# Combining the two softmax maps of a differential attention on GpSimd, in two instructions, instead of in one of VectorE

## The chip, the core and the metric

The kernel runs on one core of a Trainium2 chip. The core has a matrix engine (TensorE, PE in the profile, with its weight loads as PEld), three elementwise engines (VectorE or DVE, ScalarE or ACT, GpSimd or POOL) and SyncE (SP), which issues DMAs. TensorE writes to PSUM, which has eight banks; GpSimd works on SBUF only. The metric is the device time of one execution in microseconds (us).

## The reference, cut to what matters

One encoder block on 1024 tokens of width 1024, in float32: an input projection, two attentions side by side, gates, an output projection and an MLP. The change lies in the second attention, the differential one, with 4 heads. Its core, for each block of 128 queries:

```python
sc = jnp.einsum('bqhcd,bkhcd->bhcqk', qb, k).astype(jnp.float32) * scale
p = jax.nn.softmax(sc, axis=-1)
pd = p[:, :, 0] - lam * p[:, :, 1]
return jnp.einsum('bhqk,bkhe->bqhe', pd.astype(v.dtype), v)
```

So there are two maps of 128 queries by 1024 keys per head and block, and one is subtracted from the other with a factor before the product with the values. The heads' outputs are normalised afterwards.

## The kernel before, in words

Products are made in halves: a float32 matrix is split into a high part, which TensorE takes, and the low part that remains, and a product is three products of such parts. Making a low part is one elementwise subtraction, and which engine makes it is written in the code.

The program has stages, one behind the other: input projections, the differential attention, the dilated attention, the gates and the output projection, and the MLP in two stages. The differential attention is one loop over 34 steps, in which 4 heads of 8 query blocks each are worked on with a lag:

- `b_scores` (lines 688 to 703) makes the scores of both maps of block n on TensorE, `sb` in the rows (line 697), in a PSUM tile of two banks; there are two such tiles. VectorE takes the minimum of each row, `mn` (line 700; the sign of the scores is turned), and ScalarE the exponential, `p` (line 702), which also sums the row into `zz`.
- `b_combine` (lines 705 to 712), one step later, takes the reciprocals of the sums, `zi` (line 710), the ratio `rr` of the two sums with the factor lambda (line 711), and adds the second map, times that ratio, to the first (line 712). The map is thus left with the scale of the first sum; the normalisation later takes the reciprocal into account.
- `b_values` (lines 714 to 726), two steps later, transposes the combined map on TensorE in eight pieces, `tb` (line 724), into two PSUM tiles. `split_T` makes the high part on ScalarE (line 622) and the low part on VectorE (line 623), `pt`. Every second block `b_products` multiplies the values with the parts of two blocks, `ob` (lines 735 to 737), which ScalarE copies out (line 738).
- `fill`, at every second step, adds a piece of other work: half of a gate's projection (`gate_first`, lines 625 to 646). A weight is loaded (`wgf`), split into a high part by ScalarE (line 253) and a low part by GpSimd (line 254, `wa_g_l`), multiplied (line 245, `g`), and GpSimd adds the result to three stored parts (line 641, `gq`), on which ScalarE takes a tanh.
- `b_norm`, once a head, has a small step on GpSimd (lines 164 and 165), and near the end GpSimd makes the low halves of the next stage's weights (line 150, `wb_l`).

The order in which each engine's instructions stand is not that of the text: a scheduler places all instructions of the program, by its own estimate of their durations, and puts in the waits. Each engine then goes through its queue strictly in that order. So a changed instruction can also change where its neighbours stand, on every engine and in SP's queue of loads.

The maps `p` are in a pool of 9 tiles, the transposed parts `pt` in one of 7.

Of the kernel before, what the change touches and what calls it, by code (L numbers as in the profile page):

```python
# [14 lines left out]
ALU = mybir.AluOpType  # L15
# [68 lines left out]
def tile_hybrid_block(ctx: ExitStack, tc: tile.TileContext, t: dict, out: bass.AP):  # L84
    nc = tc.nc
# [511 lines left out]
    def tiny(tag, name, w=8, bufs=2):  # L597
        return p2.tile([P, w], F32, tag=tag, name=name, bufs=bufs)
# [106 lines left out]
    def b_combine(o, qb):  # L705
        h = o.h
        pm, zz = o.p[qb], o.zz[qb]

        r = tiny("rr", f"rr{h}_{qb}", 1, 4)
        nc.vector.reciprocal(o.zi[:, qb, :], zz)  # L710
        nc.vector.scalar_tensor_tensor(r, zz[:, 0:1], lam, o.zi[:, qb, 1:2], op0=ALU.mult, op1=ALU.mult)
        nc.vector.scalar_tensor_tensor(pm[0], pm[1], r, pm[0], op0=ALU.mult, op1=ALU.add)

    def b_values(o, qb):
        h, pr, u = o.h, qb // 2, qb % 2
# [225 lines left out]
    for n in range(len(steps) + LAG):  # L941
        if n < len(steps):
            h, qb = steps[n]
            if qb == 0:
                heads[h] = b_open(h)
            b_scores(heads[h], qb)
        if n % 2:
            fill()

        if n == 28:  # L950
            ah[0] = a_open(0)
        if n == 30:
            ah[1] = a_open(1)
        if 0 < n <= len(steps):
            h, qb = steps[n - 1]
            b_combine(heads[h], qb)
        later()
        if n >= LAG:
            h, qb = steps[n - LAG]
            defer(b_values(heads[h], qb))  # L960
            if qb == NT - 1:
                defer(partial(b_close, heads.pop(h)))
# [440 lines left out]
```

## Time and profile before

| | us |
|---|---|
| median of 3 runs | 1702.39 |
| lowest and highest | 1696.20, 1707.07 |
| the profiled execution | 1701.56 |
| its span, from first to last instruction | 1699.8 |

Busy time is what an engine spent in instructions that compute; several engines are busy at once, so the shares don't add up to one. A wait is the time that an engine was idle before an instruction, put down to what released it.

### The profile page before, as it was taken

How to read it: one execution, taken by the hardware profiler on the slowest of the kernel's cores; microseconds unless marked ns; L12 is line 12 of the kernel's file. 1: busy time of each engine (PE TensorE's matmuls, PEld its weight loads, DVE VectorE, ACT ScalarE, POOL GpSimd, SP SyncE). 2: the span in 40 equal slices, each digit the busy share in tenths (PEclk: the TensorE clock that was granted, in tenths of full speed). 3: DMA queues.
4: the chain of work that ended last, by engine and by line, in shares of the span. 5: the costliest groups of instructions: out<-in, count | busy, mean ns of one | idle time of the engine just before them, and what ended most of it. 6: DMA issues, size and time to landing. Idle time of an engine off the chain costs nothing. (4 is left out here: it accounts for less than half of the span.)

```text
span 1699.8 us, 22314 instructions
## 1 busy us (share of the span) xinstructions
PE 1569.3 (92%) x8216; PEld 1324.2 (78%) x8216; DVE 1230.8 (72%) x1560; ACT 709.4 (42%) x1176; POOL 712.4 (42%) x412
## 2 busy tenths in 40 slices
PE   7899989998889998999999998999999888999997
PEld 6798767776677778899879996777888677777776
DVE  5876788689688996555546548544344899999995
ACT  4432222222567774445422336345444643333322
POOL 1634545455223241112120016333333498888771
PEclk8999999999899998999999999999999999999999
DMA  6366576555855658665475432433332632222212
GB/s 203 130 207 211 169 227 227 166 179 175 267 192 191 230 192 276 186 203 187 144 250 184 137 96 73 147 120 115 113 112 93 248 137 99 99 100 99 87 38 99
DMA packets 211869, 272.36 MB, mean 160 GB/s; under 512 B 12304, under 2 KB 146608, under 8 KB 211760
## 3 DMA queue, kind: packets, MB, share of 16 engines
q1 hardware_dynamic: 207152, 254.16, 46.0%
q10 hardware_dynamic: 4608, 16.78, 2.5%
q8 instruction: 65, 1.06, 0.3%
q14 instruction: 44, 0.36, 0.1%
HBM read 184.86 MB, written 80.27 MB: 156 GB/s over the span
## 5 line engine op out<-in xcount | busy, mean ns | idle before, releaser
L1291 PE MATMUL p<-wb_h,fa_h 128*128 128x512 f32 x392 | 157.1, 402 | 21.5 <-DVE xb L1301 8.1
L1292 PE MATMUL p<-wb_l,fa_h 128*128 128x512 f32 x392 | 155.8, 397 | 4.2 <-DVE wb_l L1249 4.2
L1293 PE MATMUL p<-wb_h,fa_l 128*128 128x512 f32 x392 | 155.3, 397 | 0.0
L1291 PEld LDWEIGHTS p<-wb_h,fa_h 128*128 128x128 f32 x392 | 74.9, 191 | 44.4 <-issue 14.5
L1249 POOL TENSOR_TENSOR wb_l<-ws,wb_h 128x512 fp32r<-128x512 f32 x54 | 86.0, 1603 | 17.3 <-ACT wb_h L1248 17.3
L1292 PEld LDWEIGHTS p<-wb_l,fa_h 128*128 128x128 f32 x392 | 75.5, 193 | 20.7 <-DVE wb_l L1249 5.2
L1293 PEld LDWEIGHTS p<-wb_h,fa_l 128*128 128x128 f32 x392 | 75.3, 192 | 16.5 <-DVE fa_l L1249 0.5
L702 ACT ACTIVATE p<-sb,mn 128x1024 f32<-128x1024 f32 x64 | 71.4, 1117 | 38.3 <-DVE mn L700 24.1
L697 PE MATMUL sb<-kb,qb 128*128 128x512 f32 x256 | 74.7, 416 | 13.1 <-ACT p L702 7.6
L700 DVE TENSOR_REDUCE mn<-sb 128x1 f32<-128x1024 f32 x64 | 76.7, 1216 | 11.0 <-PE sb L697 10.7
L1249 POOL TENSOR_TENSOR wb_l<-w2r,wb_h 128x512 fp32r<-128x512 f32 x48 | 78.7, 1660 | 13.7 <-ACT wb_h L1248 13.7
L164 POOL TENSOR_SCALAR n_y<-n_ss 128x1 f32<-128x1 f32 x23 | 6.0, 261 | 186.1 <-ACT n_xn L171 183.1
L273 DVE TENSOR_TENSOR s<-w 128x512 f32<-128x512 f32 x15 | 13.5, 901 | 97.2 <-DMA w<-in_w_ff 97.2
L254 POOL TENSOR_TENSOR wt_f_l<-w,wt_f_h 128x1024 fp32r<-128x1024 f32 x15 | 36.1, 2408 | 91.6 <-ACT wt_f_h L253 91.6
L1248 ACT ACTIVATE fa_h<-fs 128x512 fp32r<-128x512 f32 x56 | 35.1, 627 | 84.9 <-issue 40.9
L1249 DVE TENSOR_TENSOR fa_l<-fs,fa_h 128x512 fp32r<-128x512 f32 x56 | 70.4, 1264 | 0.0
L811 PE MATMUL sa<-kh_a,zq 128*128 128x256 f32 x256 | 69.2, 301 | 0.0
L1248 ACT ACTIVATE fa_h<-fr 128x512 fp32r<-128x512 f32 x50 | 31.2, 626 | 90.7 <-PE p L1292 52.2
L836 DVE TENSOR_TENSOR pta<-ta,pta 128x512 fp32r<-128x512 f32 x64 | 43.8, 688 | 33.7 <-ACT pta L835 33.4
L697 PEld LDWEIGHTS sb<-kb,qb 128*128 128x128 f32 x256 | 46.4, 194 | 25.4 <-ACT p L702 11.2
L811 PE MATMUL sa<-kl_a,zq 128*128 128x256 f32 x256 | 66.1, 289 | 0.0
L1142 ACT ACTIVATE c<-c 128x512 f32<-128x512 f32 x64 | 39.6, 623 | 56.2 <-DVE c L300 50.1
(500 smaller groups left out, 5272.1 us busy)
## 6 DMA issues: line engine op xcount, KB each, us to landing
w<-in_w_in SPq DMA_DIRECT2D x32, 512.0 KB, 4.2
qk<-r ACTq DMA_DIRECT2D x32, 512.0 KB, 4.5
f<-c SPq DMA_DIRECT2D x64, 256.0 KB, 4.6
w2r<-in_w_ff SPq DMA_DIRECT2D x32, 512.0 KB
fr<-f SPq DMA_DIRECT2D x32, 512.0 KB, 6.2
w<-in_w_ff SPq DMA_DIRECT2D x30, 512.0 KB
vb<-vb SPq DMA_DIRECT2D x16, 512.0 KB, 6.9
rot<-raw SPq DMA_DIRECT2D x64, 128.0 KB, 3.8
```

Source lines behind the costliest of these rows:

```text
L254: eng.tensor_tensor(lo[:, :n, :], x, f(hi[:, :n, :]), op=ALU.subtract)
L697: nc.tensor.matmul(sps[:, 512 * n:512 * n + 512], q[:, z, (qb % 4) * P:(qb % 4 + 1) * P], o.k[m][:, 512 * n:512 * n + 512], start=z == 0, ...
L700: nc.vector.tensor_reduce(mn, sps, axis=AX.X, op=ALU.min)
L702: nc.scalar.activation(p, sps, AF.Exp, scale=-1.0, bias=mn, accum_out=o.zz[qb][:, m:m + 1])
L811: nc.tensor.matmul(ps[:, 0:CM], zq[:, n % 4, c, :], kk[:, c * CM:(c + 1) * CM], start=c == 0 and kk is o.kh, stop=c == NCLS - 1 and kk is ...
L836: nc.vector.tensor_tensor(view[1], tv, f(view[0]), op=ALU.subtract)
L1142: nc.scalar.activation(c, c, AF.Relu)
L1248: nc.scalar.activation(hi, x, AF.Copy)
L1249: eng.tensor_tensor(lo, x, f(hi), op=ALU.subtract)
L1291: nc.tensor.matmul(acc, ah[:, c], bh, start=i == 0, stop=False)
L1292: nc.tensor.matmul(acc, ah[:, c], bl, start=False, stop=False)
L1293: nc.tensor.matmul(acc, al[:, c], bh, start=False, stop=i == len(ops) - 1)
```

## The change

The one VectorE instruction of `b_combine` that multiplies the second map by the ratio and adds the first becomes two on GpSimd: the second map is multiplied by the ratio in place, and then the two maps are added into the first. The reciprocals and the ratio stay on VectorE.

```diff
         nc.vector.scalar_tensor_tensor(r, zz[:, 0:1], lam, o.zi[:, qb, 1:2], op0=ALU.mult, op1=ALU.mult)
-        nc.vector.scalar_tensor_tensor(pm[0], pm[1], r, pm[0], op0=ALU.mult, op1=ALU.add)
+        nc.gpsimd.tensor_scalar(pm[1], pm[1], r, None, op0=ALU.mult)
+        nc.gpsimd.tensor_tensor(pm[0], pm[0], pm[1], op=ALU.add)
```

In the rows of the order, lines behind 712 are higher by one in the changed kernel. Names have the block and the map or part in them: `p_5_0` is the first map of block 5, `rr_5` its ratio, `zi` the reciprocals of the head.

VectorE's queue in the second head, where the ratios of blocks 5 and 6 stand. Before:

```order
L711 SCALAR_TENSOR_TENSOR rr_5_4337<-zz_5_4256,lam,zi_3895 128x1
L712 SCALAR_TENSOR_TENSOR p_5_0_4264<-p_5_1_4273,rr_5_4337,p_5_0_4264 128x1024
L768 SCALAR_TENSOR_TENSOR eb_3639<-eb_3639,gsub,rrow_4165 128x1024
L623 TENSOR_TENSOR pt_1_0_1_4239<-tb_2_0_4242,pt_1_0_0_4238 128x4x128
L700 TENSOR_REDUCE mn_6_0_4324<-sb_6_0_4319 128x1
L772 TENSOR_TENSOR obl_4206<-eb_3639,obh_4205 128x1024
L623 TENSOR_TENSOR pt_1_1_1_4241<-tb_2_1_4249,pt_1_1_0_4240 128x4x128
```

And with the change:

```order
L700 TENSOR_REDUCE mn_6_1_4346<-sb_6_1_4341 128x1
L710 RECIPROCAL zi_3902<-zz_5_4268 128x2
L711 SCALAR_TENSOR_TENSOR rr_5_4350<-zz_5_4268,lam,zi_3902 128x1
L710 RECIPROCAL zi_3902<-zz_6_4331 128x2
L711 SCALAR_TENSOR_TENSOR rr_6_4443<-zz_6_4331,lam,zi_3902 128x1
L623 TENSOR_TENSOR pt_2_0_1_4382<-tb_4_0_4385,pt_2_0_0_4381 128x4x128
L623 TENSOR_TENSOR pt_2_1_1_4384<-tb_4_1_4392,pt_2_1_0_4383 128x4x128
```

The combination is gone from the queue, and the ratio of block 5 has moved behind the minima of block 6 and stands right ahead of the ratio of block 6.

GpSimd's queue around the same blocks, from the gate additions of one gate to the weight half of the next. Before:

```order
L254 TENSOR_TENSOR wa_g_l<-wgf_4554,wa_g_h 128x1024
L641 TENSOR_TENSOR gq_4281<-gq_4281,gp_7_4285 128x512 x2
L641 TENSOR_TENSOR gq_7_4283<-gq_7_4283,gp_7_4285 128x512
L254 TENSOR_TENSOR wa_g_l<-wgf_4847,wa_g_h 128x1024
L641 TENSOR_TENSOR gq_4560<-gq_4560,gp_0_4564 128x512 x2
```

And with the change:

```order
L641 TENSOR_TENSOR gq_4293<-gq_4293,gp_7_4297 128x512 x2
L641 TENSOR_TENSOR gq_7_4295<-gq_7_4295,gp_7_4297 128x512
L712 TENSOR_SCALAR p_5_1_4285<-p_5_1_4285,rr_5_4350 128x1024
L713 TENSOR_TENSOR p_5_0_4276<-p_5_0_4276,p_5_1_4285 128x1024
L712 TENSOR_SCALAR p_6_1_4348<-p_6_1_4348,rr_6_4443 128x1024
L713 TENSOR_TENSOR p_6_0_4339<-p_6_0_4339,p_6_1_4348 128x1024
L254 TENSOR_TENSOR wa_g_l<-wgf_4867,wa_g_h 128x1024
L712 TENSOR_SCALAR p_7_1_4416<-p_7_1_4416,rr_7_4502 128x1024
```

Between the gate additions and the weight half, which stood next to each other, there are now the combinations of two blocks, in the same queue.

TensorE's queue between the transposes of blocks 4 and 5 of the second head. Before:

```order
L724 MATMUL tb_4_1_4378<-ident,p_4_0_4189 128x128 x4
L697 MATMUL sb_7_0_4386<-kb_0_3875,qb_0_1_3885 128x512
L697 MATMUL sb_7_1_4395<-kb_1_3877,qb_1_1_3888 128x512 x4
L724 MATMUL tb_5_0_4433<-ident,p_5_0_4264 128x128 x4
L245 MATMUL g_0_4565<-hB_167,wa_g_h 128x512
```

And with the change:

```order
L725 MATMUL tb_4_1_4392<-ident,p_4_0_4200 128x128 x4
L697 MATMUL sb_7_0_4400<-kb_0_3882,qb_0_1_3892 128x512 x4
L697 MATMUL sb_7_1_4409<-kb_1_3884,qb_1_1_3895 128x512 x4
L245 MATMUL g_7_4418<-hB_169,wa_g_l 128x512
L725 MATMUL tb_5_0_4448<-ident,p_5_0_4276 128x128 x4
```

Between the two blocks' transposes stood one product of the first map's scores of block 7 and four of the second; now all eight stand there, and one gate product. In the third and fourth head it is the eight score products alone.

## Rows read from the trace of the kernel before

**Rows 1.** The page, first part: busy us, share of the span, instructions of each engine.

```profile
PE 1569.3 (92%) x8216; PEld 1324.2 (78%) x8216; DVE 1230.8 (72%) x1560; ACT 709.4 (42%) x1176; POOL 712.4 (42%) x412
```

**Rows 2.** Busy time by stretch: stretch, length, busy us (instructions), clock, DMA share, GB/s.

```profile
core 0: us, PE busy (x) PEld busy (x) DVE busy (x) ACT busy (x) POOL busy (x), PEclk, DMA share, GB/s
442.00:641.00 199.00, 183.09 (x1064) 155.65 (x1063) 174.61 (x245) 144.15 (x254) 67.82 (x40) 0.96 0.62 211
...
480.00:510.00 30.00, 26.93 (x147) 22.88 (x145) 23.25 (x34) 18.11 (x33) 8.08 (x6) 0.89 0.59 198
...
570.00:600.00 30.00, 26.75 (x157) 22.57 (x156) 26.62 (x35) 21.80 (x41) 9.41 (x6) 1.00 0.57 202
600.00:641.00 41.00, 37.17 (x226) 31.96 (x224) 38.16 (x55) 31.00 (x54) 17.28 (x10) 0.94 0.66 233
```

**Rows 3.** Waits, 430 to 650 us: who waited for whom, total us, times, longest.

```profile
ACT p L702 <- DVE mn L700: 24.1, 21, 3.3
...
DVE pt L623 <- ACT pt L622: 11.3, 11, 4.0
PEld sb L697 <- ACT p L702: 11.2, 12, 3.5
```

**Rows 4.** Instructions by line and shape, 430 to 650 us: columns as shown first.

```profile
line engine op names shapes xcount | busy us, mean ns | idle before us <-releasers
...
L712 DVE SCALAR_TENSOR_TENSOR p<-p,rr,p 128x1024 f32<-128x1024 f32 x32 | 41.6, 1300 | 0.8
...
L641 POOL TENSOR_TENSOR gq<-gq,gp 128x512 f32<-128x512 f32 x24 | 36.1, 1533 | 60.9 <-ACT gp L636 60.9
...
L254 POOL TENSOR_TENSOR wa_g_l<-wgf,wa_g_h 128x1024 fp32r<-128x1024 f32 x7 | 18.3, 2614 | 46.1 <-ACT wa_g_h L253 15.9 <-DMA gate<-gp 12.0 <-PE tb L724 9.9
...
L150 POOL TENSOR_TENSOR wb_l<-wb_r,wb_h 128x1024 fp32r<-128x1024 f32 x3 | 7.7, 2563 | 11.9 <-ACT wb_h L148 11.9
...
L991 POOL MEMSET pta<- 128x512 f32 x1 | 0.5, 525 | 10.4 <-PE ob L737 10.4
```

**Rows 5.** Timeline, GpSimd: start us, us, instruction [idle before, releaser].

```profile
443.48 3.77 POOL L641 TENSOR_TENSOR gq<-gq,gp 128x512 f32<-128x512 f32 x3 [17.35 <-ACT gp L636]
450.66 2.39 POOL L254 TENSOR_TENSOR wa_g_l<-wgf,wa_g_h 128x1024 fp32r<-128x1024 f32 x1 [3.41 <-ACT wa_g_h L253]
...
559.23 0.25 POOL L164 TENSOR_SCALAR nb_y<-bms 128x8 f32<-128x8 f32 x1 [9.36 <-DVE bms L756]
559.56 1.68 POOL L165 TENSOR_TENSOR nb_y<-nb_y,mhalf 128x8 f32<-128x8 f32 x1
```

**Rows 6.** Timeline, ratios on VectorE and what ran beside three of them.

```profile
484.61 1.06 ACT L253 ACTIVATE wa_g_h<-wgf 128x1024 fp32r<-128x1024 f32 x1 [4.10 <-DMA wgf<-in_w_in]
...
485.74 2.36 POOL L254 TENSOR_TENSOR wa_g_l<-wgf,wa_g_h 128x1024 fp32r<-128x1024 f32 x1 [11.98 <-DMA gate<-gp]
...
486.79 1.33 DVE L711 SCALAR_TENSOR_TENSOR rr<-zz,lam,zi 128x1 f32<-128x1 f32 x1
...
487.30 2.07 PE L697 MATMUL sb<-kb,qb 128*128 128x512 f32 x4 [3.07 <-ACT p L702]
...
492.40 0.22 DVE L711 SCALAR_TENSOR_TENSOR rr<-zz,lam,zi 128x1 f32<-128x1 f32 x1
...
617.89 2.40 POOL L150 TENSOR_TENSOR wb_l<-wb_r,wb_h 128x1024 fp32r<-128x1024 f32 x1 [5.67 <-ACT wb_h L148]
...
618.95 1.36 DVE L711 SCALAR_TENSOR_TENSOR rr<-zz,lam,zi 128x1 f32<-128x1 f32 x1
...
629.47 2.93 POOL L150 TENSOR_TENSOR wb_l<-wb_r,wb_h 128x1024 fp32r<-128x1024 f32 x1 [1.69 <-ACT wb_h L148]
...
630.72 1.70 DVE L711 SCALAR_TENSOR_TENSOR rr<-zz,lam,zi 128x1 f32<-128x1 f32 x1
```

**Rows 7.** Timeline, eight score products of TensorE in a row.

```profile
501.04 2.08 PE L697 MATMUL sb<-kb,qb 128*128 128x512 f32 x8
```

**Rows 8.** Timeline, the end of the stage.

```profile
635.81 1.06 ACT L148 ACTIVATE wb_h<-wb_r 128x1024 fp32r<-128x1024 f32 x1 [3.87 <-DMA wb_r<-in_w_branch_b]
...
640.03 1.28 DVE L712 SCALAR_TENSOR_TENSOR p<-p,rr,p 128x1024 f32<-128x1024 f32 x1
...
641.17 1.05 PE L724 MATMUL tb<-ident,p 128*128 128x128 f32 x4
```

## The prediction

> **What bounds the kernel now.** I read the page's first part [rows 1]: TensorE is busy for 92% of the span, VectorE for 72%, GpSimd for 42%. Those are averages over stages, and the change touches one stage alone, the 32 query blocks of the differential attention. So the second view is busy time by stretch. All 32 combinations lie between 442 and 641 us; in these 199 us TensorE is busy 183.09, VectorE 174.61, ScalarE 144.15 and GpSimd 67.82 [rows 2]. TensorE has 15.91 us idle in it; three of the stretches, 480 to 510, 570 to 600 and 600 to 641, hold 3.07, 3.25 and 3.83 of that. The stage is close to TensorE's work, with VectorE nearly as full behind it, and GpSimd has two thirds of its time free.
>
> The third view is the waits. The exponentials waited 24.1 us for VectorE's minima, and TensorE's weight loads of the scores then waited 11.2 us for exponentials to free their banks; VectorE in turn waited 11.3 us for ScalarE [rows 3]. So a shorter VectorE queue is worth something, at most TensorE's idle time. One piece is not VectorE's: at 484.61 us ScalarE had stood 4.10 us behind the load of a weight, and TensorE's scores then waited 3.07 us [rows 6]. That leaves 15.91 - 3.07 = 12.8 us.
>
> **What is removed.** 32 VectorE instructions of mean 1300 ns [rows 4], 41.6 us. They stand between the minima and the low halves in VectorE's queue, so this is relief for the waits above and nothing else.
>
> **What is added.** On GpSimd 32 scalings and 32 adds of 128x1024. An add of that size with two inputs takes 2.39 us when nothing disturbs it (the weights' low half at 450.66) [rows 5]. The scaling by one value per partition has no row of its size. Bounds: the fill of 128x512 took 525 ns [rows 4], so 1.05 us for twice the columns, reading nothing; the two-input operation took 2.39. The scaling reads one stream where the add reads two and the fill none; it is nearer to the fill, and I take 1.2 us, about half the add. A combination then costs 3.6 us in place of 1.28 (the free instruction at 640.03) [rows 8].
>
> By the Trainium skill, GPSIMD Engine Reference, Engine selection, elementwise work is VectorE's, about twice as fast on two inputs, while one input runs at roughly line rate on GpSimd. Its cycle accounting gives 1.03 cycles an element for small bodies, by estimate 0.9 us at 1.2 GHz for the scaling; no run here shows it, and the sum below would have GpSimd at 83% in place of 88%.
>
> GpSimd's queue now. It holds 24 gate additions (three in 3.77 us), 7 and 3 weight halves of 2.39, and three pairs of small steps of 0.25 + 1.68 [rows 4, 5]: 30.2 + 23.9 + 5.8 = 59.9 us. With 32 x 3.6 = 115.2 it is 175.1 of 199, 88%. It fits, but only just, and this queue was free of anything urgent before.
>
> **The lock between the two engines.** The step ahead of each combination, the ratio rr on VectorE, works on one column and takes 0.22 us (492.40). Three times it did not: 1.33 us from 486.79, 1.36 from 618.95, 1.70 from 630.72 [rows 6]. Each time a GpSimd instruction ran, 485.74 + 2.36 = 488.10, 617.89 + 2.40 = 620.29, 629.47 + 2.93 = 632.40, and the ratio ended 0.02 us behind it. It stands still until GpSimd's instruction is over. Now GpSimd will be in a long instruction (32 adds and 10 halves, 100.4 us) half the time and in a short one (56 of about 1.22, 68.6 us) a third of it. A ratio that arrives at random waits half an instruction: 100.4/199 x 1.2 + 68.6/199 x 0.61 = 0.82 us, over 32 ratios 26 us. VectorE's relief shrinks from 41.6 to 15.4 us, 37%, and I count 37% of 12.8: **4.8 us less**. In the new order some ratios stand right behind each other (blocks 5 and 6 of the second head): the second meets the scaling that the first has started, and the low halves behind it wait too.
>
> The Trainium skill says in SBUF — State Buffer, Who interferes with whom, that a VectorE instruction with two SBUF inputs and a GpSimd instruction that reads SBUF exclude each other for the whole instruction. The trace agrees on the ratios (ends 0.02 us apart); the page would have no share of the waits escape, which is the third rival.
>
> **The tail.** The last block has no work behind it. Its exponential ended, its combination ran from 640.03, and transposes came at 641.17 [rows 8]. There 3.6 + 0.1 - 1.28 = **2.4 us more** is on the path (2.3 by the low bound of the scaling, 3.6 by the high one).
>
> **The queue.** GpSimd's weight halves feed gate products that TensorE takes in order. Each of the 10 now finds a combination in front of it with a chance of 115/199 = 58%, with half of 3.6 us left: 1.0 us each, 10.4 in all. TensorE has scores and values ahead of half of these, by the order: **5.2 us more**. A combination behind a gate addition or a half is later too, and each is 2.3 us longer in itself. That is covered by what TensorE has between a block's transposes and the next block's: eight score products of 2.08 us [rows 7] and a share of gate or value products. The cover is thinnest between blocks 4 and 5 of the last three heads, where one gate product or none stands beside the scores; with nothing but the scores each block would cost up to 2.3 - 2.08 = 0.2 us, some 7 us over 32, which I leave to the range.
>
> The order before and behind the stage is as it was apart from a few loads on SP's queue between this stage and the next, which I cost at nothing: GpSimd and SP wait for the last products there in any case.
>
> **Sum.** Against the profiled execution's 1701.56 us: -4.8 + 2.4 + 5.2 = +2.8, or 1704.4. That execution lies 0.8 us under the median of 1702.39, so the forecast is **1705 us**, no change that can be told: a measurement of this kernel resolves about 1%, 17 us.
>
> **Rivals.**
> *VectorE's relief comes through.* If the ratios mostly arrive while GpSimd waits for them, the whole 12.8 us can return and the queue costs nothing: 1701.6 - 12.8 + 2.4 = 1691. For it: VectorE is named in the longest wait of the stage. Against it: 88% of GpSimd, and TensorE at 92%. Chance 0.15; only with the low bound of every cost is it over 1%, so 0.06 for faster.
>
> *GpSimd becomes the bound of the stage.* Place: its queue from 442 to 641 us. It decides from the scaling's price: (199 - 59.9) / 32 = 4.35 us for a combination, so a scaling over 1.95 us. At its upper bound of 2.39 the queue holds 32 x 4.78 + 59.9 = 212.9 us, 13.9 over; with the tail's 3.6 that is 1719. With 5% of idle time, since it must wait for ratios, halves from ScalarE and loads, 224 us and 1730. A late load is now paid here too: at 635.81 ScalarE had waited 3.87 us for the weight whose low half GpSimd makes [rows 8], and in the new order one such half stands between the scaling and the add of block 5 of the last head. For it: no row shows that one input is cheaper than two, and the disturbed rows are longer (2614 ns mean of the halves, 1533 of the additions) [rows 4]. Against it: what disturbed them was above all the VectorE instruction that goes. Chance 0.22.
>
> *The lock takes back more than the change gives.* If each ratio waits a whole add, 32 x (2.39 - 0.22) = 69 us, VectorE holds 174.6 - 41.6 + 69 = 202 of the 199 us and becomes the bound itself: 1701.6 + 3 + 2.4 = 1707 with no idle time, 1720 if half of its 24 us of idle time today stays. For it: ratios side by side in the order. Against it: the ratio has to precede its own combination, so the longest instruction is often still to come. Chance 0.08.
>
> The forecast keeps 0.55. That the change doesn't do what it says is excluded: the order shows the 64 instructions on GpSimd and none left on VectorE.
>
> **Range and chances.** Low end 1690, the first rival; high end 1730, the second with its idle time. Faster by over 1%: 0.06. Slower by over 1%, above 1719: most of the second rival, part of the third, and of the forecast the case that cover and tail both go wrong, 0.28. Within 1%: 0.66.
>
> **What would show it.** In the new profile: the scaling's mean (1.2 us forecast, the case turns at 1.95); GpSimd's busy time from the first to the last combination (175 of about 200 us); the ratio's mean, 0.22 us plus 0.82, about 1.04 (2.4 for the third rival); TensorE's waits for transposes, which should now name the GpSimd add, few and at block 5 of a head and the end; the exponentials' wait for minima, which should fall from 24.1 us by a third. The prediction is wrong if the stage lasts under 190 or over 215 us, or if the difference lies outside it.

## The result, and the profile after it

The changed kernel takes 1754.46 us (median of 4 runs, 1753.00 to 1755.47); the kernel before, on the same chip, 1702.14. The ratio is 1.0308, with a 95% interval of 1.0274 to 1.0342: **slower by 3.1%**, 52 us. The forecast was 1705, with a range of 1690 to 1730. The profiled execution has a span of 1753.7 us, 53.9 more than before.

The first part of the page, which answers to [rows 1]:

```profile
PE 1590.4 (91%) x8216; PEld 1338.4 (76%) x8216; DVE 1213.4 (69%) x1528; ACT 709.1 (40%) x1176; POOL 874.1 (50%) x476
```

GpSimd has gained 161.7 us for 64 instructions, 5.05 per combination. VectorE has lost 32 instructions, but only 17.4 us of the 41.6 that they took [rows 4].

Busy time by stretch. The combinations now lie between 439 and 695 us, 256 where it was 199 [rows 2]:

```profile
439.00:695.00 256.00, 206.54 (x1089) 171.79 (x1088) 155.12 (x217) 145.18 (x257) 228.38 (x103) 0.89 0.53 176
```

For a measure with the same work on both sides I take the time from the first score product of this stage to the first of the next: 222.4 us before and 274.5 after, 52.1 more, all but 1.8 of the difference of the spans. The rows of these two stretches, before and after:

```profile
432.00:654.00 222.00, 203.10 (x1160) 172.27 (x1161) 185.80 (x259) 150.95 (x265) 69.74 (x44) 0.95 0.66 222
```

```profile
430.00:704.00 274.00, 222.03 (x1161) 183.67 (x1160) 164.20 (x228) 150.04 (x264) 230.31 (x107) 0.89 0.54 179
```

The last three columns are TensorE's granted clock, the DMA share and GB/s. No engine is full: GpSimd is busy for 84% of it, TensorE for 81%. Of the 52 us, 33.1 are more idle time of TensorE, and in the other 18.9 it is busy longer with the same products, at a granted clock of 0.89 in place of 0.95.

The instructions on GpSimd, from the page (last number: idle time ahead of them), and VectorE's ratios, grouped by line:

```profile
L712 POOL TENSOR_SCALAR p<-p,rr 128x1024 f32<-128x1024 f32 x32 | 91.2, 2850 | 34.5 <-DMA vb<-vb 16.0
...
L713 POOL TENSOR_TENSOR p<-p,p 128x1024 f32<-128x1024 f32 x32 | 76.1, 2380 | 2.1
```

```profile
L711 DVE SCALAR_TENSOR_TENSOR rr<-zz,lam,zi 128x1 f32<-128x1 f32 x32 | 23.1, 721 | 1.3
```

The scaling, which reads one map, costs **2850 ns**, more than the addition, which reads two (2380). A combination is 5.23 us in place of 1.30. The ratio's mean is 721 ns.

The waits from 430 to 704 us, as in [rows 3]:

```profile
ACT p L702 <- DVE mn L700: 46.1, 22, 14.2
DVE zi L710 <- ACT p L702: 39.8, 18, 10.3
...
ACT gq L644 <- POOL gq L641: 29.2, 12, 7.4
PEld tb L725 <- POOL p L713: 24.6, 11, 5.4
...
PE tb L725 <- POOL p L713: 19.6, 8, 5.0
PE sb L697 <- ACT p L702: 17.9, 15, 3.3
...
POOL p L712 <- DVE rr L711: 11.6, 9, 5.0
...
PE row_nb L616 <- DVE stat L761: 5.1, 2, 3.9
```

And in the kernel before, from 430 to 650 us, those rows that [rows 3] doesn't have:

```profile
ACT p L702 <- DMA qb<-qk: 14.2, 1, 14.2
...
PE sb L697 <- ACT p L702: 7.6, 6, 3.1
...
ACT gq L644 <- POOL gq L641: 5.7, 5, 1.9
...
DVE zi L710 <- ACT p L702: 2.6, 4, 1.2
...
PE row_nb L616 <- DVE stat L760: 0.6, 1, 0.6
```

The first row of each list holds the same wait of 14.2 us, that of the first exponential of the stage; before the change it is put down to a load. Without it the exponentials' wait for minima rose from 24.1 [rows 3] to 31.9 us. TensorE waited 19.6 us for additions of the combination, which had no such row before, 10.3 us more for exponentials, and 4.5 more for the row of the normalisation (`row_nb`).

The waits after the change name a ring: VectorE waits for exponentials, ScalarE for minima and for GpSimd's sums, TensorE for GpSimd's additions and for exponentials, GpSimd for ratios. Two places show how it is held. In the first, TensorE stands for a block's combination (GpSimd's timeline, VectorE's, TensorE's; start us, us, instruction [idle before]):

```profile
610.40 5.67 POOL L712 TENSOR_SCALAR p<-p,rr 128x1024 f32<-128x1024 f32 x2 [1.13 <-DVE rr L711]
616.04 4.65 POOL L713 TENSOR_TENSOR p<-p,p 128x1024 f32<-128x1024 f32 x2
```

```profile
609.99 0.21 DVE L711 SCALAR_TENSOR_TENSOR rr<-zz,lam,zi 128x1 f32<-128x1 f32 x1
```

```profile
618.43 1.97 PE L725 MATMUL tb<-ident,p 128*128 128x128 f32 x8 [4.95 <-POOL p L713]
```

The ratio ended at 610.20, but the transposes began 8.2 us later, not 5.2: the scaling of the next block stands between the scaling and the addition of this one. TensorE, whose queue has these transposes next, was idle for 4.95 us. From the starts and ends of all 32 in the two timelines, the way from the end of a ratio to the end of its addition is 7.7 us on average (5.4 to 13.2): 5.2 for the two instructions, 2.0 ahead of the scaling and 0.5 between the two. Of the time ahead of the scaling, 62 us over the 32, GpSimd spent 43 in scalings and additions of other blocks, 11 in gates' sums and 5 in weight halves. Before the change the way was 1.7 us. The transposes then began 7.1 us behind the combination on average (0.4 to 14.9), and in the change 4.2; within 0.6 us of its end they began in 2 of the 32 blocks before, in 11 after.

In the second, a gate's sums stand around the addition, and ScalarE behind them (GpSimd, ScalarE, TensorE):

```profile
567.57 2.85 POOL L712 TENSOR_SCALAR p<-p,rr 128x1024 f32<-128x1024 f32 x1
570.38 1.26 POOL L641 TENSOR_TENSOR gq<-gq,gp 128x512 f32<-128x512 f32 x1
571.60 2.35 POOL L713 TENSOR_TENSOR p<-p,p 128x1024 f32<-128x1024 f32 x1
573.91 2.51 POOL L641 TENSOR_TENSOR gq<-gq,gp 128x512 f32<-128x512 f32 x2
```

```profile
571.67 0.63 ACT L644 ACTIVATE gq<-gq 128x512 f32<-128x512 f32 x1 [7.36 <-POOL gq L641]
572.21 1.10 ACT L702 ACTIVATE p<-sb,mn 128x1024 f32<-128x1024 f32 x1
...
576.45 0.63 ACT L644 ACTIVATE gq<-gq 128x512 f32<-128x512 f32 x1 [0.60 <-POOL gq L641]
576.99 1.10 ACT L702 ACTIVATE p<-sb,mn 128x1024 f32<-128x1024 f32 x1
```

```profile
563.18 2.09 PE L697 MATMUL sb<-kb,qb 128*128 128x512 f32 x8
...
573.45 1.68 PE L697 MATMUL sb<-kb,qb 128*128 128x512 f32 x4 [3.29 <-ACT p L702]
578.23 2.08 PE L697 MATMUL sb<-kb,qb 128*128 128x512 f32 x4 [3.10 <-ACT p L702]
```

The exponential at 572.21 had nothing to do with the gate, but ScalarE's queue has the tanh of the sum ahead of it, and the sum stood behind the scaling. TensorE then waited 3.29 and 3.10 us for that exponential and the next to free their banks. Behind the second wait four products took the 2.08 us in which eight ran at 563.18: the granted clock from 578.2 to 580.4 us was 0.50, the lower of its two levels, 1.2 in place of 2.4 GHz.

### The profile page after: what moved, and what is told of

Read it like the earlier page. It is cut to its first block, busy times and chain, and to the rows that moved or that the text cites. A ratio compares the mean times of both kernels' runs of the same rounds, so it can differ in the third digit from the quotient of the medians.

```text
span 1753.7 us, 22413 instructions
## 1 busy us (share of the span) xinstructions
PE 1590.4 (91%) x8216; PEld 1338.4 (76%) x8216; DVE 1213.4 (69%) x1528; ACT 709.1 (40%) x1176; POOL 874.1 (50%) x476
## 5 line engine op out<-in xcount | busy, mean ns | idle before, releaser
L712 POOL TENSOR_SCALAR p<-p,rr 128x1024 f32<-128x1024 f32 x32 | 91.2, 2850 | 34.5 <-DMA vb<-vb 16.0
L697 PE MATMUL sb<-kb,qb 128*128 128x512 f32 x256 | 81.4, 447 | 23.4 <-ACT p L702 17.9
L1250 POOL TENSOR_TENSOR wb_l<-ws,wb_h 128x512 fp32r<-128x512 f32 x54 | 85.7, 1596 | 17.4 <-ACT wb_h L1249 17.4
L697 PEld LDWEIGHTS sb<-kb,qb 128*128 128x128 f32 x256 | 50.0, 211 | 39.0 <-ACT p L702 24.5
L713 POOL TENSOR_TENSOR p<-p,p 128x1024 f32<-128x1024 f32 x32 | 76.1, 2380 | 2.1
L623 DVE TENSOR_TENSOR pt<-tb,pt 128x512 fp32r<-128x512 f32 x64 | 42.3, 684 | 35.9 <-ACT pt L622 35.8
```

The source lines that it names most:

```text
L697: nc.tensor.matmul(sps[:, 512 * n:512 * n + 512], q[:, z, (qb % 4) * P:(qb % 4 + 1) * P], o.k[m][:, 512 * n:512 * n + 512], start=z == 0, ...
L712: nc.gpsimd.tensor_scalar(pm[1], pm[1], r, None, op0=ALU.mult)
L713: nc.gpsimd.tensor_tensor(pm[0], pm[0], pm[1], op=ALU.add)
L1250: eng.tensor_tensor(lo, x, f(hi), op=ALU.subtract)
```

## Experiments

My first theory was the prediction's second rival: the scaling is dear, and GpSimd's total load is the bound. Its rivals: the lock between VectorE and GpSimd; and the length of a combination in a ring of queues that each run strictly in order. Every time below is a median; each ratio is to the kernel before on the same chip, with its 95% interval.

**The prices alone** (`e1_prices`): a small kernel that runs each operation four times or more on 128x1024 in SBUF, with nothing beside it.

> Computes nothing of the block: it runs single operations on 128x1024 tiles, four of each, on GpSimd with no other engine beside it, to price them. Theory 1 (the scaling by one value per partition is dear in itself): 2.85 us in place, as in the changed kernel, and the same into another tile; the add 2.39. Theory 2 (the scaling is made dear by what runs beside it in the stage): 1.0 to 1.3 us here. By a fixed number as factor, and over 512 and 256 columns: no forecast by theory 2; by theory 1 the time goes with the columns, 1.45 and 0.75 us. Multiplying by a broadcast column as a two-input operation: 2.39 by both.

Instructions by line and shape (busy us, mean ns | idle before):

```profile
L28 POOL TENSOR_SCALAR a<-a,r 128x1024 f32<-128x1024 f32 x4 | 11.4, 2845 | 4.1 <-DMA a<-in_x 3.8
...
L30 POOL TENSOR_SCALAR a<-a 128x1024 f32<-128x1024 f32 x4 | 11.1, 2770 | 0.3
...
L39 POOL TENSOR_TENSOR b<-b,a 128x1024 f32<-128x1024 f32 x4 | 9.4, 2340 | 0.1
L37 POOL TENSOR_TENSOR a<-a,r 128x1024 f32<-128x1024 f32 x4 | 7.6, 1893 | 0.3
L35 POOL TENSOR_SCALAR a<-a,r 128x512 f32<-128x512 f32 x4 | 6.3, 1565 | 0.4
...
L41 POOL COPY c<-a 128x1024 f32<-128x1024 f32 x4 | 4.2, 1039 | 0.0
L35 POOL TENSOR_SCALAR a<-a,r 128x256 f32<-128x256 f32 x4 | 3.7, 925 | 0.4
L43 DVE TENSOR_SCALAR a<-a,r 128x1024 f32<-128x1024 f32 x4 | 3.0, 753 | 70.2 <-POOL c L41 70.1
```

The scaling's 2.85 us are its own, undisturbed, also with a fixed number (2770). A two-input multiplication with the ratio spread over the columns is cheaper (1893); VectorE scales in 753. The three widths lie on a line: 2.5 ns a column and 0.285 us besides.

**Half the blocks, the addition alone, the cheaper scaling** (`e2_half`, `e3_add_only`, `e4_broadcast`).

```diff
+        if qb % 2:                      # e2_half; else: VectorE's one instruction
             nc.gpsimd.tensor_scalar(pm[1], pm[1], r, None, op0=ALU.mult)
             nc.gpsimd.tensor_tensor(pm[0], pm[0], pm[1], op=ALU.add)
```
```diff
-        nc.gpsimd.tensor_scalar(pm[1], pm[1], r, None, op0=ALU.mult)    # e3_add_only
```
```diff
-        nc.gpsimd.tensor_scalar(pm[1], pm[1], r, None, op0=ALU.mult)    # e4_broadcast
+        nc.gpsimd.tensor_tensor(pm[1], pm[1], r.to_broadcast([P, S]), op=ALU.mult)
```

> Every second block is combined on GpSimd, the others on VectorE as before. Theory Q (GpSimd's queue is what the stage waits for, 228 of 256 us): the queue falls to 16 x 5.23 + 61 = 145 us, well under the 199 us of the stage before, and the time goes back to 1695 to 1712 us. Theory L (each combination is late by its own length, 5.3 us in place of 1.3, whatever the queue holds): half of the 52 us stays, 1728 us. Theory K (the lock takes VectorE's time): half of it stays too, since half of the GpSimd time that locks is there, 1728 us.

> The scaling is left out, so the second map is added unscaled; GpSimd makes the 32 adds alone. Theory Q: GpSimd holds 32 x 2.38 + 61 = 137 us of 199 and bounds nothing, 1693 to 1708 us. Theory L: a combination is 1.1 us longer than on VectorE where it was 4.0 longer in the change, 27% of 52 us, 1716 us. Theory K: the locking time of GpSimd falls from 228 to 137 us, so 60% of the loss stays, 1733 us.

> The scaling on GpSimd is a two-input multiplication by the ratio's column, broadcast over the columns, in place of the operation with a value per partition. Theory Q: 0.46 us less for each of 32 in the queue, 15 us less, 1740 us. Theory L: 0.46 of the 4.0 us of lateness goes, 6 us, 1748 us. If the broadcast multiplication costs the same as the scaling, no change from 1754 us.

Measured: half 1715.39 (1.0086, 1.0055 to 1.0117); addition alone 1720.68 (1.0115, 1.0081 to 1.0150); cheaper scaling 1725.59 (1.0141, 1.0107 to 1.0176). The half lies above the range of the load theory and well under the 1728 us of the others; the addition alone comes nearest to the 1716 of the length theory. The last is 28.9 us under the change for 32 x 0.957 = 30.6 us less of GpSimd's work, nearly one to one; its expectation took 0.46 us for the saving, where it is 0.96.

But with the addition alone GpSimd is busy for 139.65 of 240 us, and the kernel is still 20 us slower; load can't be the reason there. Nor can the length of the combination. The additions don't wait for the ratio, and from the end of a block's second exponential to the end of its addition it is 3.0 us on average, less than the 4.4 to the end of the combination in the kernel before; the transposes begin 9.2 us behind it, later than the 7.1 before. TensorE's waits there, from 430 to 670 us:

```profile
PE row_nb L616 <- DVE stat L760: 8.4, 3, 2.8
...
PE tb L724 <- POOL p L712: 1.3, 1, 1.3
```

It hardly waits for additions (1.3 us, 19.6 in the change). The wait that grew most is that for the row of the normalisation (0.6 us before), on whose way GpSimd has a small step. Most of the ratios met an addition (median 1990 ns, least 204; 45.1 us in all, 10.8 before), and the lock became a suspect.

**The lock** (`e5_ratio_one_input`): the ratio by an instruction that reads one tensor and two values per partition.

```diff
-        nc.vector.scalar_tensor_tensor(r, zz[:, 0:1], lam, o.zi[:, qb, 1:2], op0=ALU.mult, op1=ALU.mult)
+        nc.vector.tensor_scalar(r, zz[:, 0:1], lam, o.zi[:, qb, 1:2], op0=ALU.mult, op1=ALU.mult)
```

> The changed kernel, but the ratio on VectorE is an operation with one tensor and two values per partition in place of one with two tensors. In the changed kernel the 32 ratios took 23.1 us in place of 7, because they stood still behind GpSimd. Theory K (that lock is a good part of the 52 us): if the ratios now take 0.2 us each, 16 us of VectorE's time return and 10 to 20 us of the total, 1735 to 1745 us. Theory Q (GpSimd's queue bounds the stage, with 5.23 us for each combination): GpSimd gains nothing, 1749 to 1756 us. If the ratios stay long, one tensor doesn't avoid the lock and nothing follows.

All ratios of the run by line: duration ns min/median/max, first and last start:

```profile
L711 DVE TENSOR_SCALAR rr<-zz,lam,zi x32: 265/272/277, 442.4 to 686.6; 128x1 f32<-128x1 f32 x32
```

No ratio is held up any more, and the time is 1751.51 (1.0297, 1.0271 to 1.0324), 3 us under the change. The lock on the ratio is not where the 52 us went. With the addition alone, where it held the ratios for 34 us more than before, this edit wasn't tried, so the lock stays open as a cause of those 20 us. In the kernel before, the same edit gave nothing:

> The kernel before, with the ratio by VectorE's instruction with one tensor and two values per partition. GpSimd's few instructions hold up the ratio now and then in the kernel before (32 take 10.8 us where 7.0 would do), and this form was never held up (272 ns each, 8.7 us): VectorE gains 2 us at most. If the ratio's hold-up mattered: 1699 to 1701; otherwise the same as before within 0.2%.

Measured: 1702.97 against 1703.59 (1.0000, 0.9984 to 1.0015).

**GpSimd's load** (`e8_gates_on_vector`): the gates' additions and low weight halves go to VectorE.

```diff
-        a11, a12 = halves(ra, f"wa_g{n}")
+        a11, a12 = halves(ra, f"wa_g{n}", nc.vector)
-            nc.gpsimd.tensor_tensor(c, c, p, op=ALU.add)
+            nc.vector.tensor_tensor(c, c, p, op=ALU.add)
```

> The changed kernel, with GpSimd's other work of the stage, 24 gate additions and 8 weight halves, on VectorE. Theory Q: GpSimd's queue falls from 228 to about 175 us, 51 us less, and the time falls by 30 to 50 us, to 1705 to 1725 (VectorE takes about 25 us more than its 164 of 274 and is no bound). Theory L (the length of a combination alone): nothing changes for a block but a queue without strangers, 1740 to 1754 us. Theory K: the time that GpSimd locks falls by 23%, 12 us, 1742 us.

Measured: 1749.54 (1.0289, 1.0267 to 1.0310), 5 us under the change, though GpSimd's work fell from 230 to 189 us. The load theory fell here, as the only reason at least (VectorE is busy for 28 us more in return). The waits of this run:

```profile
POOL p L712 <- DVE rr L711: 42.0, 11, 8.7
...
PE tb L725 <- POOL p L713: 24.7, 10, 4.3
```

GpSimd now stands idle for ratios, and TensorE still waits for its additions. That gave the theory of the combination's length, and two ways to shorten the way round it without any change in GpSimd's work.

**More room for the combination**: one step more between scores and transposes (`LAG = 3`, from 2), for the half, the kernel before, the change, and the change with the gates on VectorE; or the ratio earlier in VectorE's queue, by calling `b_combine` of the block before ahead of `b_scores`.

```diff
-    LAG = 2
+    LAG = 3
```
```diff
+        if 0 < n <= len(steps):          # ahead of b_scores; behind fill() before
+            h, qb = steps[n - 1]
+            b_combine(heads[h], qb)
```

> Every second block on GpSimd, as in the run that came out at 1715 us, and the transposes of a block one step later in the program (a lag of three steps in place of two). Theory L for what is left there (GpSimd is not full, 147 of 237 us, but each of its combinations is late for the transposes; TensorE waited 10 us for them): the wait goes and the time is within 6 us of the kernel before with the same lag. If the 15 us come from the lock or the order, they stay.

> The kernel before, with the lag of three steps: the control for the run with half of the blocks. No theory of the change bears on it; the combination on VectorE is early enough with two steps, so 1695 to 1706 us is expected, or a few us more for the longer end of the stage.

> The changed kernel, with the call that combines block n-1 placed ahead of the call that makes the scores of block n, so that the ratios stand further ahead in VectorE's queue: 13 of 32 ratios now stand behind one or two minima that don't belong to their block, each, where it was 2 for 9 of them and 1 for 8; the pairs scaling, scaling, addition, addition on GpSimd disappear but for two. GpSimd's work is the same. Chain theory (what sets the stage is the length of the way ratio, scaling, addition, transposes in queues that are in order): 5 to 20 us shorter than the change, 1735 to 1750. Load theory (GpSimd's total of 229 us sets it): no change, 1752 +- 4.

> The changed kernel with a lag of three steps instead of two between a block's scores and its transposes, so that a combination has one step (6 to 8 us) more before TensorE wants it. Same instructions and the same load of GpSimd. The same step for the kernel before cost 10 us, for the half version 2. Chain theory: the waits of TensorE for GpSimd's addition (19.6 us, its weight loads 24.6) go, the stage comes down from 274 to 240 to 250 us (GpSimd's 229 with small gaps), time 1720 to 1735. Load theory: no shorter than the change, 1750 to 1765.

> The gates' additions and low weight halves on VectorE (as in the run before with 1749.5), and the ratios early as in the other kernel of this call; GpSimd then has 189 us of work and a queue that alternates scaling and addition without anything between. Chain theory: the wait of GpSimd for the ratio falls from 42 us to under 20, the stage from 269 to 240 to 255, time 1722 to 1737. If the total over GpSimd and VectorE under the lock sets it (the additions moved to VectorE are held up), no change: 1745 to 1755.

> The gates' additions and low weight halves on VectorE, and the lag of three steps. GpSimd has 189 us of work. Chain theory: with neither a short way nor a full queue the stage comes down to 225 to 238 us (the kernel before with this lag: 231.5), time 1705 to 1722, some 10 to 15 us under the changed kernel with the lag of three alone, which has GpSimd full. If the lock or VectorE's additional 40 us set it: over 1735.

> Control: the kernel before with the call of the combination ahead of the scores, all on VectorE. The 9 us that this gave to the changed kernel and the 24 us that it gave beside the moved gates should not be a gain of the order as such: 1698 to 1708, same.

Measured, in us, with the kernel before beside them (median 1700.61 to 1703.59):

| | lag 2 | early ratio | lag 3 |
|---|---|---|---|
| kernel before | 1702.14 | 1704.32 | 1710.92 |
| half of the blocks | 1715.39 | | 1717.87 |
| the change | 1754.46 | 1743.52 | 1761.10 |
| the change, gates on VectorE | 1749.54 | 1725.39 | 1715.77 |

(Ratios: early 1.0003, 0.9988 to 1.0019, for the kernel before, 1.0239, 1.0205 to 1.0273, for the change, and 1.0152, 1.0113 to 1.0191; lag 3 1.0050, 1.0028 to 1.0072, then 1.0111, 1.0084 to 1.0139, then 1.0346, 1.0312 to 1.0380, and 1.0082, 1.0053 to 1.0111.) With the gates' work away, the room is worth 24 and 34 us, where it costs the kernel before 2 and 9. The lag alone (1761) gives nothing, the lower load alone (1750) 5 us, the early ratio alone 11; lag and lower load together leave 5 us over the control at that lag. The half lost TensorE's 10.3 us of waiting for additions with the lag, and stayed 7 us over that control, a little more than the 6 expected. The control itself, at 1711, came out 5 us over its range. The change with lag 3 missed the 1720 to 1735 of the chain theory and lies in the range of the load theory. TensorE's waits for additions were nearly gone from its list (1.9 us); this stood at its head:

```profile
ACT gq L644 <- POOL gq L641: 45.8, 15, 4.9
```

**ScalarE behind the gates' sums, or the load?** (`e13_tanh_free`, `e14_tanh_free_lag3`): GpSimd does the same additions, into a tile that nobody reads.

```diff
-            nc.gpsimd.tensor_tensor(c, c, p, op=ALU.add)
-        nc.vector.tensor_tensor(p, acc, p, op=ALU.add)
+            nc.gpsimd.tensor_tensor(scr, scr, p, op=ALU.add)
+        p0, p = p, p2b.tile([P, 512], F32, tag="gfr", name=f"gfr{n}")
+        nc.vector.tensor_tensor(p, acc, p0, op=ALU.add)
```

> The changed kernel, in which GpSimd's 24 additions of the gates go into a tile that nobody reads, and ScalarE takes the tanh of the three stored parts without their addend (so the gates lack this addend); VectorE's sum goes into a tile of its own. GpSimd has the same instructions and the same 230 us of work, but ScalarE no longer waits for it (29.2 us in the change, ahead of exponentials in its queue). Two-wait theory (the stage is set by ScalarE's queue behind GpSimd's sums and by TensorE's queue behind GpSimd's combination, and either alone holds it): 1740 to 1755, as when the gates' work was moved away (1749.5). If ScalarE's wait alone is the cause: 1715 to 1735.

> The same without ScalarE's wait for the gates' sums, and with the lag of three steps (with the wait: 1761.1; with the gates' work on VectorE: 1715.8). GpSimd keeps its 230 us. Two-wait theory: both waits are gone, and the stage comes down to GpSimd's work with gaps, 240 to 252 us, time 1718 to 1735. Load theory (it was the 40 us less on GpSimd that brought the 45 us): 1750 to 1765.

Measured: 1754.56 with lag 2 (1.0292, 1.0260 to 1.0323; its runs lie between 1744.91 and 1756.20), 1737.92 with lag 3 (1.0207, 1.0187 to 1.0226). So ScalarE's wait alone is worth nothing that can be told, and with the room 23 us of the 45, at the same load; 1737.92 lies between the two expectations. For the rest the load is the nearest reason, as the middle of that stage shows (columns as above):

```profile
460.00:660.00 200.00, 166.01 (x941) 142.08 (x939) 133.85 (x184) 122.92 (x215) 193.69 (x90) 0.90 0.54 173
```

GpSimd is busy for 193.69 of 200 us: here it is nearly full. In the change it was 178.00 in the same stretch.

A third waiter shows here, which none of my theories had. The normalisation's small step stands in the same queue (GpSimd's timeline, VectorE's, TensorE's):

```profile
586.53 2.34 POOL L716 TENSOR_TENSOR p<-p,p 128x1024 f32<-128x1024 f32 x1
588.84 0.24 POOL L164 TENSOR_SCALAR nb_y<-bms 128x8 f32<-128x8 f32 x1
589.16 1.67 POOL L165 TENSOR_TENSOR nb_y<-nb_y,mhalf 128x8 f32<-128x8 f32 x1
```

```profile
578.32 0.15 DVE L760 TENSOR_TENSOR bms<-ms,ba 128x8 f32<-128x8 f32 x1
...
590.87 0.17 DVE L762 TENSOR_TENSOR nb_y<-nb_y,zi 128x8 f32<-128x8 f32 x1 [8.94 <-POOL nb_y L165]
```

```profile
591.30 0.47 PE L616 MATMUL row_nb<-ident,stat 128*128 128x128 f32 x1 [8.79 <-DVE stat L764]
```

Its input was ready at 578.47, but it began at 588.84, behind a weight half and combinations; VectorE and TensorE, each in its order, stood idle for 8.94 and 8.79 us. From 430 to 690 us TensorE waited 18.9 us for this row, its longest item. No run moved this step, so what it is worth isn't measured.

**The price again, in both settings** (`e17_scaling_at_forecast_price`, `e18_tanh_free_lag3_cheaper_scaling`).

```diff
-        nc.gpsimd.tensor_scalar(pm[1], pm[1], r, None, op0=ALU.mult)    # e17, in the change
+        nc.gpsimd.tensor_scalar(pm[1][:, 0:512], pm[1][:, 0:512], r, None, op0=ALU.mult)
```

(The other run has the two-input scaling of `e4_broadcast` in the kernel of `e14_tanh_free_lag3`.)

> The changed kernel with the scaling on the first 512 columns alone (the other half of the second map is added unscaled), so that it costs what the prediction took for the whole, 1.33 us by the run of prices, 1.2 in the prediction. GpSimd's work falls from 230 to about 182 us, what the prediction counted (175). If the scaling's price was the only step that failed: 1700 to 1710, the forecast. If the length of the combination on GpSimd and ScalarE's queue behind it count as well: between the run with the addition alone (1720.7) and the one with the cheaper scaling (1725.6), 1716 to 1726.

> The run with the tanh freed and the lag of three (1737.9), in which GpSimd was busy 193.7 of 200 us in the middle of the stage, with the scaling as a multiplication of two inputs (1.89 us in place of 2.85), in nearly the same order. If GpSimd's work was what held that run: its time falls by up to 32 x 0.96 = 31 us, until the next bound, the kernel before with this lag (1710.9): 1710 to 1718. If something else held it (the waits that the lag brings, the order): 1728 to 1740.

Measured: 1723.92 (1.0131, 1.0110 to 1.0151) and 1722.47 (1.0134, 1.0105 to 1.0163). The first by line on GpSimd:

```profile
L712 POOL TENSOR_SCALAR p<-p,rr 128x512 f32<-128x512 f32 x32 | 50.2, 1570 | 39.6 <-DVE rr L711 32.2 <-DVE ba L756 3.8 <-ACT wb_h L148 3.3
```

With a scaling of 1570 ns, a third over the 1.2 us of the forecast, the change still costs 22 us. (The 1.33 us of the expectation was misread; the run of prices had 1565 ns for 512 columns.) It has the load of the run with the gates on VectorE (191 against 189 us of GpSimd's work) and a combination shorter by 1.2 us, and is 26 us faster than that run, so GpSimd's load alone doesn't set the time. (The two also differ by 25 us of work on VectorE, so the 26 need not be the length's alone; with the same work on VectorE but earlier ratios the other run came down to 1725.39, its way from ratio to addition from 7.4 to 6.7 us on average.) The price also saturates: from 2850 to 1893 ns it gave 28.9 us, from there to 1570 another 1.7, and without any scaling 3.2 more, which is hardly clear of the noise. The second run fell by 15 of the 31 us, between its two expectations: GpSimd nearly was the bound of that kernel, but half way down it was no longer full (162.69 of 180 us from 460 to 640). What held it from there is not settled; TensorE's longest wait, from 430 to 680 us, is again for the row of the normalisation, 10.7 us in four pieces.

No version came under the kernel before, and none of the numbers points to one: with half of the blocks, the scaling left out, or both waits relieved, each stays 13 us or more above it.

## Why the prediction was wrong

**The place was right.** All but 1.8 of 53.9 us lie in the stage, which lasted 256 us where the prediction's own bound for being wrong was 215.

**First step that failed: the price of the scaling.** The prediction took 1.2 us between bounds of 1.05 and 2.39, "nearer to the fill". It measured 2.85, outside both ends. The upper end was the mistake: the two-input addition was taken as the most that a one-input operation can cost, and no row supported that. By the Trainium skill, GPSIMD Engine Reference, Engine selection, one input runs at roughly line rate; the estimate from its cycle accounting was 0.9 us. GpSimd's copy comes near it (1039 ns), the scaling does not by three times, and the measurement decides. By the halved scaling, 1.28 of the 1.65 us beyond the forecast's price are worth 1754.46 - 1723.92 = 30.5 us.

**Second step that failed: the cover.** "Covered by what TensorE has between a block's transposes and the next block's" was worked out for a block by itself: 2.3 us longer against scores of 2.08 [rows 7], nothing in the sum. The queues don't treat a block by itself: other instructions of GpSimd add 2.5 us to a combination's own 5.2, and the way from the ratio to the end of the addition grew by 6.1 us on average, nearly the 7.1 that lay between the combination and its transposes before. TensorE waited 19.6 us for additions. The order of the changed kernel showed these neighbours; a way counted along it from a ratio to its transposes, block after block, would have shown more than 2.3. With the halved scaling the way still grew by 3.4 us (to 5.0), and TensorE waited 8.0 us for additions. That is part of the 22 us that remain there, where the sum had +2.8. How the rest of them divides stays open: the addition alone costs 20 us with hardly any such wait. The lock on VectorE, the normalisation's row, and the order in which the scheduler then places the neighbours were not told apart.

**The queue term (5.2 us)** asked only who waits for GpSimd's weight halves. TensorE has no wait for one in the stage. The waiters were others: ScalarE's tanh behind the gates' sums, ahead of exponentials (29.2 us, 5.7 before), and the normalisation's row. The first alone decides nothing (1754.56 without it); beside the combination's length it is a second hold (1737.92 against 1761.10, both with the lag of three).

**The lock term was twice too large on the ratios, and not the cause.** The prediction let the lock take back 26 of 41.6 us, all on the ratios. VectorE's busy time fell by 17.4 over the program, so 24.2 came back, but only 12.3 of them on the ratios (10.8 us before, 23.1 after); that the total is near 26 is luck. The ratio's mean of 1.04 us was forecast, 721 ns came. An example of both rows (GpSimd, VectorE):

```profile
593.19 2.39 POOL L713 TENSOR_TENSOR p<-p,p 128x1024 f32<-128x1024 f32 x1
```

```profile
594.01 1.58 DVE L711 SCALAR_TENSOR_TENSOR rr<-zz,lam,zi 128x1 f32<-128x1 f32 x1
```

The ratio ends at 595.59, 0.01 us behind the addition. The Trainium skill, SBUF — State Buffer, Who interferes with whom, gives the lock to VectorE's operations with two SBUF inputs; the ratio with one tensor was never held up (at most 277 ns), which agrees. Since removing it from the ratios gave 3 us, it has no share worth naming there; on other instructions of VectorE it wasn't removed.

**The relief (-4.8 us) never came.** The exponentials' wait for minima was to fall by a third from 24.1 [rows 3]; it rose to 31.9. In VectorE's queue the minima stand behind reciprocals that wait for exponentials (39.8 us, 2.6 before), and in TensorE's the scores behind transposes.

**The tail (+2.4 us)** was 4.3: the last ratio ended at 688.71 and the transposes came at 694.22, 5.5 us, where it had been some 1.2 [rows 8]. Nearly all of the excess is the scaling's price.

**The second rival**, GpSimd as the bound (0.22, up to 1730), had the sign, the place and a load sum that holds: with the measured prices 32 x 5.23 + 59.9 = 227 us, and 228.38 came. By its own rule, with 5% of idle time and the tail of 4.3, that is some 1746, 8 us short. It is part of the cause. The full load, with two of the waits out of the way, gives 1737.92 (at lag 3, which costs the kernel before 9 us); the waits, with 189 us of load, 1749.54; the change has both and needs 1754.46. What is not settled is how the 52 us divide between the two, since they are not additive: relieving one uncovers the other. The scaling's price is in both, which fits that 30.6 us less of it gave 28.9.

## What to carry to other kernels

A price without a row of its own operation has no upper bound from a neighbour that looks heavier; measure it, or let the range reach beyond it. Where a step moves to an engine that other engines wait for, count the way from its input to its reader along the new order of that engine's queue, with every instruction that stands between, and list every waiter of the work that it delays, down to the small steps. When two such holds stand beside each other, taking one away can show next to nothing (1750, 1761); take both away (1716) before calling either innocent.

## What the hardware showed that I had not expected

GpSimd's scaling by one value costs 2845 ns for 1024 columns, 1565 for 512 and 925 for 256, that is 2.5 ns a column and 0.285 us besides. It is dearer than the two-input addition (2340) and half again as dear as the two-input multiplication with a spread operand (1893), while the copy takes 1039.

And a lower granted clock adds to what waits cost: the same products of the stage took 203.10 us at a clock of 0.95 and 222.03 at 0.89, so more than a third of the stage's 52 us is not idle time at all. That the waits brought the lower clock is not shown; with the tanh freed TensorE was busy for only 208.89 of 273 us, and the clock was 0.91.
